# A folded matrix stored by partition, a single row's products moved back, and two order edges in the opening

## The chip, the cores and the metric

The kernel runs on one core of one Trainium2 chip. The metric is device microseconds of one execution, from the median of several runs. The engines are called as in the profile: PE (TensorE, matmuls), ACT (ScalarE), DVE (VectorE), POOL (GpSimd) and SP (SyncE, which issues nearly all DMAs).

## The reference

One step of a two-layer backbone on 256 context tokens and 1024 latent tokens (10 tiles of 128) of width 1024. Each layer normalises its input, modulates it by shift and scale from the condition, mixes, gates and adds:

```
h = modulate(rms_norm(x, g), shift, scale)      # shift, scale, gate = silu(c) @ W_ada + b
even layer: p = h @ W_in; mixer A global GQA, mixer B windowed GQA with a sink,
            x = x + gate * ([silu(gA)*A, silu(gB)*B] @ W_out)
odd layer:  u = h @ W_u; Y = Re(FFT2(u over positions and each group's 256 channels))
            x = x + gate * ((silu(g) * Y) @ W_out)
```

Layer 0 is even, layer 1 odd; a last RMS norm gives the outputs, beside the new keys and values. All is float32.

## The kernel before, in words

All matrix products are made of a high and a low half of each operand, rounded so that PE takes them in its faster float32 form: three matmuls per product (hi·hi, hi·lo, lo·hi; `mm3`, L262 to L271). A raw float32 tile is cast to its high half on ACT or DVE (L290, L292) and the low half is a subtraction on DVE or POOL (L296); the helper is `split`.

The Fourier layer's transform over channels is folded into the weight ahead of time: W_u times the Fourier matrix of a group (tiles `wa`, L575). That product is written in the opening to a DRAM tensor `wd` and read back late, in the u stage. `wd` is laid out as [2, 1024, 2, 256]: half, row of the matrix, group, column. `fold_put` (L563 to L565) writes four 128-row blocks at a time; each partition gets pieces of 1 KB, which lie 2 KB apart from one partition to the next.

**The opening** (0 to about 70 us). Four `warm` matmuls on zeros (L233) come first. Then PE folds `wa`, computes the chunks `ada0` to `ada3` of the condition's linear map (L488), transposes normalised x tiles (`xt`, L445) and begins the first projections (`kv..s`, L544, and `q`, L271). The order in which the program issues these steps is a list of codes written by hand, `PH0` and `S1`; a scheduler sorts each engine's instructions from there by their waits. The steps that matter here:

- `N1` (`norm_rows`, L433 to L439): for each x tile of the second token group, ACT squares it and sums the squares (L433), DVE and POOL make the reciprocal root for two tiles at a time (`n11rx`, L248, `n11ry`, L250), and DVE scales the rows (L439).
- `A1` (`ada_chunk`, L488 to L529): 32 matmuls of a chunk, then ACT copies the resulting row from PSUM (L529). `M1` (`ada_fin`) has PE transpose that row (`modt`, L534) and DVE add and multiply it into `modb` and `moda` (L500, L505, L506).
- `Y2` (`mod_chunk`, L452 to L460): a transposed chunk of x becomes a modulated high and low half: ACT writes the high one (L458), DVE the full value (L459) and the difference (L460).
- `s1`: the splits of the weight `w1` (`w_in`), whose raws are `h` tiles: casts at L292, differences at L296.

SP's DMAs use eight semaphores in turn, and an issue waits until the DMA eight before it has landed.

**The u stage** (about 970 to 1000 us). For each of the two halves of `wd`, `u_load` reads four raw tiles per half and column part (L1565, two DMAs each of 128x2x129 or 128x2x128), splits them, and PE computes blocks `u00` to `u04`, then `u10` to `u14`, of 24 matmuls of 128x258 each (L271). One token position stands alone (the Nyquist row); its products with the same raw tiles are `xr`, 16 matmuls per half in four groups of four (L1578). A raw tile's buffer is free once its high half, low half and `xr` group have read it.

Of the kernel before, what the change touches and what calls it, by code (L numbers as in the profile page):

```python
# [9 lines left out]
F32 = mybir.dt.float32  # L10
# [3 lines left out]
AF = mybir.ActivationFunctionType  # L14
ALU = mybir.AluOpType
AX = mybir.AxisListType

P = 128
D = 1024
# [32 lines left out]
USES = ((0,), (1,), (2, 3), (2, 3), (4, 7), (6, 7), (4, 6), (5,), (8,), (9,))  # L52
BETWEEN = {(8, 1): [("E", k) for k in range(3)], (9, 0): [("E", k) for k in range(3, 8)], (9, 1): [("O", k) for k in range(2)]}
OPRE = 2
WARM = 4
BEHIND = {7: 5}
ROWS_BEHIND = (9,)
PW1 = "11111"
# [84 lines left out]
def hybrid_step(ctx: ExitStack, tc: tile.TileContext, I, O):  # L143
    nc = tc.nc
    pe, act, dve, pool, sp = nc.tensor, nc.scalar, nc.vector, nc.gpsimd, nc.sync
# [44 lines left out]
    vd = dr.tile([2, NT, P, P], F32, name="vd")  # L190
    od = dr.tile([NT, P, 8, P], F32, name="od")
    gd = dr.tile([NT, P, 8, P], F32, name="gd")
    wd = dr.tile([2, D, 2, 256], F32, name="wd")
    x1d = dr.tile([NT * P, D], F32, name="x1d")
    g1d = dr.tile([8, P, NT * P], F32, name="g1d")
    scd = dr.tile([NT, 2, 8, P], F32, name="scd")
# [67 lines left out]
    def mm3(out, terms, lo=0, hi=None):  # L264
        n = 3 * len(terms)
        hi = n if hi is None else hi
        i = 0
        for lh, ll, rh, rl in terms:
            for a, b in ((lh, rh), (lh, rl), (ll, rh)):
                if lo <= i < hi:  # L270
                    pe.matmul(out, a, b, start=i == 0, stop=i == n - 1)  # L271
                i += 1

    turn = {}
    lows = {}
# [11 lines left out]
    def copy(key, cycle, out, in_):  # L287
        e = pick(key, cycle)
        if e is act:
            return act.activation(out, in_, AF.Copy)  # L290
        else:
            e.tensor_copy(out, in_)  # L292

    def split(dst_h, dst_l, src, hc="a", lc="p"):
        copy("hi" + hc, hc, dst_h, src)
        return pick("lo" + lc, lc).tensor_sub(dst_l, src, dst_h)  # L296


# [38 lines left out]
    def wk(w, k, c0, n):  # L337
        h, l = w[k // 4]
        return h[:, k % 4, c0 : c0 + n], l[:, k % 4, c0 : c0 + n]
# [111 lines left out]
    def mod_chunk(gi, k, src, full, hh, hl, lc):  # L451
        v = GROUPS[gi][2]  # L452
        sc, sh = moda[:, 0, k, v : v + 1], modb[:, 0, k, v : v + 1]
        if pick("mf", E_MF) is act:
            act.activation(full, src, AF.Identity, bias=sh, scale=sc)
            pick("mh", E_MH).tensor_copy(hh, full)
        else:
            act.activation(hh, src, AF.Identity, bias=sh, scale=sc)  # L458
            dve.tensor_scalar(full, src, sc, sh, op0=ALU.mult, op1=ALU.add)  # L459
        pick("ml" + lc, lc).tensor_sub(hl, full, hh)  # L460

    def h_alloc(gi):
# [57 lines left out]
    def ada_chunk(kk, raws):  # L520
        ps = bank("g", f"ada{kk}")
        for b in range(8):
            for j in range(4):
                part, i = divmod(j, 2)
                raw = raws[b // 4 * 2 + part]
                ada_mm(ps, j, b, raw[:, b % 4, i * P : i * P + P], b == 0, b == 7)
        drop(*raws)
        rows[kk] = take("e", (P, P))
        act.activation(rows[kk].a, ps[:, 0:P], AF.Copy)  # L529

    def ada_fin(kk):
        row = rows.pop(kk)
# [29 lines left out]

    def fold_put(g, r0, src):  # L563
        n = src.shape[1]
        sp.dma_start(wd[g // 2, r0 : r0 + n * P, g % 2, :].rearrange("(k p) f -> p k f", p=P), src)  # L565

    early = {}

# [64 lines left out]
    def first_step(op):  # L633
        nm, i = op[0], int(op[1:])
        if nm == "L":
            ada[i] = ada_load(i, ADA_Z[i])
        elif nm == "S":
            small_loads(i)
        elif nm == "x":
            load_x(i, XZ[i])  # L640
        elif nm == "N":
            norm_rows(i)
        elif nm == "w":
            W[i] = load_w(w0cols((C_KA, C_QA)[i]), lc=LC0, later=w_fin.setdefault(i, []))
        elif nm == "s":
            for fin in w_fin[i]:
                fin()
        elif nm == "f":
            wu0[i] = fold_load(i)
        elif nm == "F":  # L650
            fold_piece(i // 10, i % 10, wu0[i // 10], True)
        elif nm == "G":
            e = early.pop((i // 10, i % 10))
            fold_put(i // 10, i % 10 * 512, e.a)
            drop(e)
        elif nm == "A":
            ada_chunk(i, ada.pop(i))
        elif nm == "M":
            ada_fin(i)
        elif nm == "T":  # L660
            XT[0, i] = x_T(0, i)
        elif nm in "XYZ":
            g = "XYZ".index(nm)
            mod_T(g, i, E_ML[g])
        elif nm in "KR":
            t = 4 * "KR".index(nm)
            gemm_chunk(acc0[t], t, W[0], i)
            gemm_chunk(acc0[t + 2], t + 2, W[0], i)
        else:
            return False  # L670
        return True
# [651 lines left out]
    def eo_cols(key, k, c0, n):  # L1323
        kper = 4 if key == "C" else 2
        hh, hl = EH[key][k // kper]
        return hh[:, k % kper, c0 : c0 + n], hl[:, k % kper, c0 : c0 + n]
# [232 lines left out]

    def u_gap(c, hf):  # L1560
        def fn(raw, r0):
            v = raw.a.rearrange("p j (g f) -> p j g f", g=2)
            cols = slice(0, 129) if c == 0 else slice(128, 256)
            for g in range(2):
                sp.dma_start(v[:, :, g, :], wd[hf, r0 : r0 + 2 * P, g, cols].rearrange("(j p) f -> p j f", p=P))  # L1565
            if c == 1:
                pool.memset(v[:, :, :, 0:1], 0.0)
        return fn

    def u_load(n):  # L1570
        c, hf = divmod(n, 2)
        ps = t_bank(f"xr{hf}") if c == 0 else None

        def row(raw, k0):
            for kk in range(2):
                for h in range(2):
                    j = 2 * kk + h
                    pe.matmul(  # L1578
                        ps[32 * j : 32 * j + 32, 0:130], xo[:, k0 + kk, :], raw[:, kk, 128 * h : 128 * h + 130],
                        start=k0 == 6, stop=k0 == 4,  # L1580
                    )
            if k0 == 4:
                act.activation(xsum[hf].a, ps[:, 0:130], AF.Copy)

        if c == 0:
            return load_w(None, width=258, tags=("u", "w", "p"), gap=u_gap(c, hf), each=row)
        return load_w(None, tags=BIG, gap=u_gap(c, hf))
# [105 lines left out]
    for n in range(4):  # L1693
# [60 lines left out]
        for i in (0, 1, 2, 3, 4):  # L1754
            if i < 4:
                key, c0 = "EO"[c], i * P
            else:
                key, c0 = "C", c * P
            ps = next_bank(f"u{n}{i}")[:, 0:width]
            mm3(ps, [(*eo_cols(key, k, c0, P), *wk(w, k, 0, width)) for k in range(8)])  # L1760
            pv = ps.rearrange("p (g f) -> p g f", g=2)
            for gg in range(2):
                hi, lo = y_at(c, i, 2 * hf + gg)
                act.activation(hi, pv[:, gg, 0:P], AF.Copy)
                dve.tensor_sub(lo, pv[:, gg, 0:P], hi)
            if c == 0:
                dve.tensor_copy(nyr[:, i, 2 * hf : 2 * hf + 2].unsqueeze(2), pv[:, :, P : P + 1])
            if n == 3 and i in AT_F:
                fine_part(AT_F.index(i))
# [242 lines left out]
```

## Time and profile before

| | us |
|---|---|
| median of 3 runs | 1184.28 (1183.18 to 1186.94) |
| profiled execution, its own time | 1181.38 |
| its span, first to last instruction | 1179.6 |
| PE busy | 1152.3 |
| DVE busy | 834.6 |
| ACT busy | 570.6 |
| POOL busy | 327.9 |

The profile is of one execution. Busy time counts an engine's own instructions; PE's is the sum that the end of the kernel follows most closely, so the reading below goes by the places at which PE waits. In a timeline row the first number is the start in us from the span's beginning, the second the duration; then engine, line of the source, operation, what it writes and reads, the count of instructions merged in the row, and in brackets the idle time before it with the instruction that ended it.

### The profile page before, as it was taken

How to read it: one execution, taken by the hardware profiler on the slowest of the kernel's cores; microseconds unless marked ns; L12 is line 12 of the kernel's file. 1: busy time of each engine (PE TensorE's matmuls, PEld its weight loads, DVE VectorE, ACT ScalarE, POOL GpSimd, SP SyncE). 2: the span in 40 equal slices, each digit the busy share in tenths (PEclk: the TensorE clock that was granted, in tenths of full speed). 3: DMA queues.
4: the chain of work that ended last, by engine and by line, in shares of the span. 5: the costliest groups of instructions: out<-in, count | busy, mean ns of one | idle time of the engine just before them, and what ended most of it. 6: DMA issues, size and time to landing. Idle time of an engine off the chain costs nothing.

```text
span 1179.6 us, 22036 instructions
## 1 busy us (share of the span) xinstructions
PE 1152.3 (98%) x8111; PEld 1033.8 (88%) x8111; DVE 834.6 (71%) x1995; ACT 570.6 (48%) x1149; POOL 327.9 (28%) x293
## 2 busy tenths in 40 slices
PE   9999999999999999999999989999999999999997
PEld 7787999999999998899988888888777889998886
DVE  3479787877677776668888968886765963468543
ACT  4343465566556555556776665532363234342211
POOL 2345644511322221010110035366221236100001
PEclk9999999999999999999999999999999999999999
DMA  9968412223523232255253487784214426264321
GB/s 367 370 240 270 153 54 76 88 83 99 162 68 102 77 96 76 79 126 134 71 155 89 133 230 222 234 253 161 90 45 145 150 98 195 85 218 141 125 108 54
DMA packets 112848, 168.81 MB, mean 143 GB/s; under 512 B 26202, under 2 KB 63830, under 8 KB 112740
## 3 DMA queue, kind: packets, MB, share of 16 engines
q1 hardware_dynamic: 110228, 158.74, 42.9%
q0 software_dynamic: 2368, 8.39, 2.3%
q8 instruction: 64, 1.05, 0.4%
q14 instruction: 44, 0.36, 0.1%
q10 hardware_dynamic: 144, 0.26, 0.1%
HBM read 123.19 MB, written 44.16 MB: 142 GB/s over the span
## 4 chain that ended last, share of the span: by engine, by line
PE 73%; DMA 11%; DVE 7%; issue 3%; ACT 2%; POOL 2%; SPq 1%; POOLq 0%; DVEq 0%; ACTq 0%
PE of L271 9%; PE av L1071 9%; PE pt L1065 8%; PE q L271 8%; PE ga L271 8%; PE sL L946 5%; PE u L271 4%; PE g1O L271 4%; PE oz L271 3%; PE g1E L271 3%; PE sC L946 3%; PE kv L271 2%; PE g1c L271 2%; DMA u<-i_x 2%; DMA wd<-u 2%
## 5 line engine op out<-in xcount | busy, mean ns | idle before, releaser
L1068 DVE TENSOR_TENSOR pt<-pt,pt 128x512 fp32r<-128x512 f32 (+1 forms) x264 | 171.2, 658 | 41.5 <-ACT pt L290 40.5
L290 ACT ACTIVATE pt<-pt 128x512 fp32r<-128x512 f32 (+1 forms) x265 | 147.2, 576 | 101.1 <-PE pt L1065 55.6
L1071 PE MATMUL av<-pt,u 128*128 128x256 f32 x1008 | 167.1, 288 | 0.7 <-ACT pt L290 0.6
L1065 PE MATMUL pt<-identr,p 128*128 128x128 f32 x1008 | 155.2, 272 | 0.6 <-ACT p L987 0.3
L271 PE MATMUL q<-w,u 128*128 128x256 f32 x960 | 143.2, 287 | 0.0
L1071 PEld LDWEIGHTS av<-pt,u 128*128 128x128 f32 x1008 | 138.7, 189 | 4.9 <-ACT pt L290 0.8
L271 PEld LDWEIGHTS q<-w,u 128*128 128x128 f32 x960 | 126.8, 189 | 5.2 <-issue 0.6
L987 ACT ACTIVATE p<-p,nm 128x1280 f32<-128x1280 f32 (+1 forms) x80 | 95.5, 1194 | 63.0 <-DVE p L980 62.4
L1065 PEld LDWEIGHTS pt<-identr,p 128*128 128x128 f32 x1008 | 119.1, 140 | 7.1 <-PE sB L1018 0.6
L271 PE MATMUL ga<-u,w 128*128 128x512 f32 (+1 forms) x576 | 124.5, 361 | 0.8 <-DVE byp L1042 0.5
L271 PEld LDWEIGHTS ga<-u,w 128*128 128x128 f32 x576 | 93.8, 188 | 15.1 <-ACT pt L290 1.2
L296 POOL TENSOR_TENSOR w<-h,w 128x512 fp32r<-128x512 f32 x38 | 50.7, 1351 | 130.4 <-DVE w L292 101.0
L946 PE MATMUL sL<-u,q 128*128 128x512 f32 x256 | 82.5, 409 | 0.0
L987 ACT ACTIVATE p<-p,NM 128x640 f32<-128x640 f32 (+2 forms) x80 | 59.2, 740 | 33.4 <-DVE p L980 33.2
L946 PE MATMUL sC<-u,q 128*128 128x256 f32 x320 | 62.8, 295 | 1.2 <-DMA q<-qd 0.6
L980 DVE TENSOR_SCALAR_CACHE_REDUCE p<-sL 128x512 f32<-128x512 f32 x64 | 43.8, 685 | 24.6 <-PE sL L946 15.1
L721 POOL TENSOR_TENSOR h<-h,rope 128x512 f32<-128x512 f32 (+1 forms) x18 | 21.8, 1212 | 125.8 <-ACT h L804 77.2
L271 PE MATMUL oz<-u,w 128*128 128x512 f32 x192 | 55.9, 396 | 0.3 <-DVE w L296 0.3
L980 DVE TENSOR_SCALAR_CACHE_REDUCE p<-sL,nm 128x512 f32<-128x512 f32 x64 | 47.7, 745 | 10.3 <-PE sL L946 9.5
L946 PEld LDWEIGHTS sC<-u,q 128*128 128x128 f32 x320 | 48.5, 189 | 4.7 <-DVE e L1082 1.0
L296 POOL TENSOR_TENSOR u<-h,u 128x512 fp32r<-128x512 f32 x16 | 21.0, 1323 | 110.1 <-ACT u L290 83.4
L271 PE MATMUL of<-u,u 128*128 128x512 f32 x150 | 48.2, 393 | 0.0
(730 smaller groups left out, 2598.5 us busy)
## 6 DMA issues: line engine op xcount, KB each, us to landing
q<-qd SPq DMA_DIRECT2D x80, 256.0 KB
h<-i_w_in SPq DMA_DIRECT2D x40, 256.0 KB
h<-i_w_out SPq DMA_DIRECT2D x32, 256.0 KB
p<-i_ada_s SPq DMA_DIRECT2D x11, 512.0 KB
qd<-pt SPq DMA_DIRECT2D x20, 256.0 KB
qd<-q SPq DMA_DIRECT2D x18, 256.0 KB
w<-i_wuT SPq DMA_DIRECT2D x8, 512.0 KB
u<-i_x SPq DMA_DIRECT2D x8, 512.0 KB
```

Of the source, the lines that this page charges most:

```text
L271: pe.matmul(out, a, b, start=i == 0, stop=i == n - 1)
L290: return act.activation(out, in_, AF.Copy)
L296: return pick("lo" + lc, lc).tensor_sub(dst_l, src, dst_h)
L721: pick("rope", XE["rope"]).tensor_mul(t1.rearrange("p t h (b c) -> p t (h b) c", b=2), y.rearrange("p t h (b c) -> p t (h b) c", b=2), cb)
L946: pe.matmul(ps, q_at(q, s, hc), keys, start=s == 0, stop=s == 1)
L980: dve.tensor_scalar(p[i][:, end[i] : end[i] + n], ps, sign, last[i], op0=ALU.mult, op1=ALU.min, accum_out=c)
L987: act.activation(p[i][:, 0 : end[i]], p[i][:, 0 : end[i]], AF.Exp, bias=last[i], scale=-1.0, accum_out=SU[:, t, hd + i, 0:1],)
L1065: pe.transpose(tp[:, jj * 256 + i * P : jj * 256 + i * P + P], p[i][:, off : off + P], ident)
L1068: dve.tensor_sub(pt[:, 1, 0:n], tp[:, 0:n], pt[:, 0, 0:n])
L1071: pe.matmul(acc, vv, pt[:, s, jj * 256 : jj * 256 + 256], start=c + jj + s == 0, stop=c + jj == nt - 1 and s == 1,)
```

## The change

Five edits, made together.

1. `WARM` goes from 4 to 6: two more matmuls on zeros at the start.
2. `wd` is laid out as [2, 128, 8, 2, 256]: half, partition, row block, group, column. The writes hold the same bytes and pieces; a partition's share of a half is now one stretch of 16 KB. `u_gap` loads a raw tile by one DMA of 128x4x129 (or 128) instead of two of 128x2x129: 16 loads instead of 32, with the same pieces of about 512 bytes.
3. The single row's products stand on PE behind the last matmul of block `u03` (first half) and `u11` (second half). `queue_behind` sets the order on an engine without adding a semaphore.
4. In the opening, ACT's copy of chunk 1's row stands behind the square of x tile (1,1).
5. In the opening, DVE's full value of the modulated chunk (1,2) stands behind the last cast of `w1`.

The helpers `mm3`, `copy`, `split` and `mod_chunk` return or remember the instructions that the order is hung on.

```diff
-WARM = 4
+XROW_BEHIND = ((0, 3), (1, 1))
+WARM = 6
...
-    wd = dr.tile([2, D, 2, 256], F32, name="wd")
+    wd = dr.tile([2, P, 8, 2, 256], F32, name="wd")
...
     def split(dst_h, dst_l, src, hc="a", lc="p"):
-        copy("hi" + hc, hc, dst_h, src)
+        lows["hi"] = copy("hi" + hc, hc, dst_h, src)
...
-            dve.tensor_scalar(full, src, sc, sh, op0=ALU.mult, op1=ALU.add)
+            lows["mc", gi, k] = dve.tensor_scalar(full, src, sc, sh, op0=ALU.mult, op1=ALU.add)
...
-        act.activation(rows[kk].a, ps[:, 0:P], AF.Copy)
+        cp_ = act.activation(rows[kk].a, ps[:, 0:P], AF.Copy)
+        if kk == 1:
+            queue_behind(cp_, lows["sq", 1, 1])
...
-        sp.dma_start(wd[g // 2, r0 : r0 + n * P, g % 2, :].rearrange("(k p) f -> p k f", p=P), src)
+        sp.dma_start(wd[g // 2, :, r0 // P : r0 // P + n, g % 2, :], src)
...
         elif nm == "s":
             for fin in w_fin[i]:
                 fin()
+                if i == 1:
+                    queue_behind(lows["mc", 1, 2], lows["hi"])
...
-            v = raw.a.rearrange("p j (g f) -> p j g f", g=2)
             cols = slice(0, 129) if c == 0 else slice(128, 256)
-            for g in range(2):
-                sp.dma_start(v[:, :, g, :], wd[hf, r0 : r0 + 2 * P, g, cols].rearrange("(j p) f -> p j f", p=P))
+            rows = wd[hf, :, r0 // P : r0 // P + 2, :, cols].rearrange("p j g f -> p (j g) f")
+            sp.dma_start(raw.a.rearrange("p j (g f) -> p (j g) f", g=2), rows)
...
-                    pe.matmul(
-                        ps[32 * j : 32 * j + 32, 0:130], xo[:, k0 + kk, :], raw[:, kk, 128 * h : 128 * h + 130],
-                        start=k0 == 6, stop=k0 == 4,
+                    xrow_mm[hf].append(
+                        pe.matmul(
+                            ps[32 * j : 32 * j + 32, 0:130], xo[:, k0 + kk, :], raw[:, kk, 128 * h : 128 * h + 130],
+                            start=k0 == 6, stop=k0 == 4,
+                        )
                     )
...
-            mm3(ps, [(*eo_cols(key, k, c0, P), *wk(w, k, 0, width)) for k in range(8)])
+            last = mm3(ps, [(*eo_cols(key, k, c0, P), *wk(w, k, 0, width)) for k in range(8)])
+            if (n, i) in XROW_BEHIND:
+                for mm in xrow_mm[n]:
+                    queue_behind(mm, last)
```

The order of instructions on an engine shows what moved. First ACT in the opening, before: `e_471<-ada_438` is the copy of chunk 1's row, the lines L433 are the squares of the second group's x tiles (u_299 to u_302).

```order
22 L455 ACTIVATE h_371<-xt_360,modb,moda 128x512
23 L433 ACTIVATE h_389,n10q<-u_299 128x1024
24 L529 ACTIVATE e_471<-ada_438 128x128
25 L433 ACTIVATE h_391,n10q<-u_300 128x1024
26 L433 ACTIVATE h_402,n12q<-u_301 128x1024
27 L433 ACTIVATE h_404,n12q<-u_302 128x1024
```

And now, with line numbers two higher and buffer numbers two higher:

```order
22 L457 ACTIVATE h_373<-xt_362,modb,moda 128x512
23 L435 ACTIVATE h_391,n10q<-u_301 128x1024
24 L435 ACTIVATE h_393,n10q<-u_302 128x1024
25 L531 ACTIVATE e_473<-ada_440 128x128
26 L435 ACTIVATE h_404,n12q<-u_303 128x1024
27 L435 ACTIVATE h_406,n12q<-u_304 128x1024
```

The copy stands one square later. On DVE the first addition of `modt` (modb) follows it: before it stood ahead of the two row scalings at L439, now behind them.

Second, DVE at `w1`, before: `h_650` is the full value of chunk (1,2), `u_644` its low half, and the casts L292 of h_571 to h_579 are the high halves of `w1`.

```order
46 L460 TENSOR_TENSOR u_526<-h_532,u_525 128x512
47 L459 TENSOR_SCALAR h_650<-xt_645,moda,modb 128x512
48 L292 CAST w_569<-h_571 128x512
49 L292 CAST w_569<-h_573 128x512
50 L460 TENSOR_TENSOR u_644<-h_650,u_643 128x512
51 L292 CAST w_575<-h_577 128x512
52 L296 TENSOR_TENSOR w_570<-h_573,w_569 128x512
53 L292 CAST w_575<-h_579 128x512
54 L500 TENSOR_TENSOR modb<-modt_659,bT 128x4
```

And now:

```order
46 L462 TENSOR_TENSOR u_528<-h_534,u_527 128x512
47 L294 CAST w_571<-h_573 128x512
48 L294 CAST w_571<-h_575 128x512
49 L298 TENSOR_TENSOR w_572<-h_575,w_571 128x512
50 L294 CAST w_577<-h_579 128x512
51 L294 CAST w_577<-h_581 128x512
52 L461 TENSOR_SCALAR h_652<-xt_647,moda,modb 128x512
53 L462 TENSOR_TENSOR u_646<-h_652,u_645 128x512
54 L502 TENSOR_TENSOR modb<-modt_661,bT 128x4
```

All four casts stand ahead of the chunk's two instructions.

Third, PE in the u stage, before: `xr_12106` is the first half's single row; u_12190, u_12222, u_12252 and u_12282 are the blocks u00 to u03, u_12119 and u_12120 the high and low halves of the raws w_12121 and w_12126.

```order
4961 L271 MATMUL u_12282<-u_12120,u_10896 128x258
4962 L271 MATMUL u_12282<-u_12119,u_10897 128x258
4963 L1578 MATMUL xr_12106<-w_12126,e_12088 32x130 x4
4964 L1578 MATMUL xr_12106<-pt_12109,e_12088 32x130 x4
4965 L1578 MATMUL xr_12106<-q_12114,e_12088 32x130 x4
4966 L1578 MATMUL xr_12106<-w_12121,e_12088 32x130 x4
4967 L271 MATMUL u_12190<-u_12119,u_10920 128x258
4968 L271 MATMUL u_12222<-u_12119,u_10920 128x258
4969 L271 MATMUL u_12252<-w_12107,w_10817 128x258
```

And now, where u_12276 is block u03 and u_12306 block u04:

```order
5005 L272 MATMUL u_12276<-u_12120,u_10922 128x258
5006 L272 MATMUL u_12276<-u_12119,pt_10923 128x258
5007 L1586 MATMUL xr_12108<-w_12125,e_12090 32x130 x4
5008 L1586 MATMUL xr_12108<-pt_12111,e_12090 32x130 x4
5009 L1586 MATMUL xr_12108<-q_12115,e_12090 32x130 x4
5010 L1586 MATMUL xr_12108<-w_12121,e_12090 32x130 x4
5011 L272 MATMUL u_12306<-w_12109,u_11078 128x258
5012 L272 MATMUL u_12306<-u_12110,u_11078 128x258
```

The row's products stand behind the end of blocks u00 to u03 instead of in their midst. On POOL the two low halves of the tile pair u_12338 (2.53 us in the trace of before under the name u<-h x2) now stand ahead of the low half u_12120 of w_12121, and on SP the loads of the second half's raws pt, q and w wait for the row's products to have read the old tiles.

More of the change, by code (lines that the diff above doesn't have):

```diff
@@ L270, in mm3 @@
                 if lo <= i < hi:
-                    pe.matmul(out, a, b, start=i == 0, stop=i == n - 1)
+                    last = pe.matmul(out, a, b, start=i == 0, stop=i == n - 1)
                 i += 1
+        return last
     turn = {}
@@ L291, in copy @@
         else:
-            e.tensor_copy(out, in_)
+            return e.tensor_copy(out, in_)
     def split(dst_h, dst_l, src, hc="a", lc="p"):
-        copy("hi" + hc, hc, dst_h, src)
+        lows["hi"] = copy("hi" + hc, hc, dst_h, src)
         return pick("lo" + lc, lc).tensor_sub(dst_l, src, dst_h)
@@ L1561, in fn @@
         def fn(raw, r0):
-            v = raw.a.rearrange("p j (g f) -> p j g f", g=2)
             cols = slice(0, 129) if c == 0 else slice(128, 256)
-            for g in range(2):
-                sp.dma_start(v[:, :, g, :], wd[hf, r0 : r0 + 2 * P, g, cols].rearrange("(j p) f -> p j f", p=P))
+            rows = wd[hf, :, r0 // P : r0 // P + 2, :, cols].rearrange("p j g f -> p (j g) f")
+            sp.dma_start(raw.a.rearrange("p j (g f) -> p (j g) f", g=2), rows)
             if c == 1:
-                pool.memset(v[:, :, :, 0:1], 0.0)
+                pool.memset(raw.a.rearrange("p j (g f) -> p j g f", g=2)[:, :, :, 0:1], 0.0)
         return fn
+    xrow_mm = ([], [])
     def u_load(n):
```

## The prediction

> **What bounds the kernel now.** I read the page's busy shares first, then the table of windows, then the timeline of the engine that is busiest, and only then the other engines at the places where that one stands still. The first line gives busy time, share of the span and instructions.
>
> ```profile
> PE 1152.3 (98%) x8111; PEld 1033.8 (88%) x8111; DVE 834.6 (71%) x1995; ACT 570.6 (48%) x1149; POOL 327.9 (28%) x293
> ```
>
> Of a span of 1179.6 us PE stands still for 27.3, so an edit that leaves PE's arithmetic alone can win only where those 27 us lie, or where PE runs below its clock. The windows show where (each row: window, its length, busy us of PE, PEld, DVE, ACT and POOL with counts, granted clock, DMA share, GB/s).
>
> ```profile
> 30.00:50.00 20.00, 18.08 (x263) 14.93 (x252) 9.07 (x23) 9.35 (x17) 6.40 (x5) 1.00 1.04 406
> 50.00:60.00 10.00, 9.73 (x120) 7.98 (x118) 6.38 (x10) 1.33 (x3) 3.75 (x3) 1.00 0.82 290
> 60.00:70.00 10.00, 8.37 (x68) 8.00 (x69) 6.64 (x12) 5.85 (x9) 5.41 (x5) 1.00 0.97 377
> 70.00:100.00 30.00, 30.00 (x373) 27.40 (x376) 26.28 (x73) 14.12 (x29) 13.15 (x16) 1.00 0.62 207
> 100.00:130.00 30.00, 26.91 (x362) 23.36 (x353) 25.87 (x61) 7.02 (x16) 19.82 (x18) 1.00 0.74 241
> ```
>
> PE loses 1.9, 0.3 and 1.6 us in the windows from 30 to 70, nothing from 70 to 100, 3.1 after 100. DMA is full from 30 to 50 us (1.04), so no load there can come sooner. PE's timeline names the stops of the opening (start, duration, work, then in brackets the idle time and who ended it).
>
> ```profile
> 1.26 3.78 PE L233 MATMUL warm<-e 128*128 128x256 f32 x8 [1.26 <-DVE ones L209]
> 5.57 6.73 PE L575 MATMUL wa<-h,w 128*128 128x256 f32 x19 [0.53 <-DMA w<-i_wuT]
> ...
> 40.95 0.41 PE L445 MATMUL xt<-identr,u 128*128 128x128 f32 x2 [1.75 <-DVE moda L505]
> ...
> 56.80 0.73 PE L544 MATMUL kv4s<-w,u 128*128 128x256 f32 x4 [0.24 <-DVE u L460]
> ...
> 61.40 0.66 PE L445 MATMUL xt<-identr,u 128*128 128x128 f32 x4 [1.44 <-ACT h L455]
> ```
>
> Their sum is 3.96 us, and each has one part of the change aimed at it. The other place is the u stage, where the single row's products stop PE twice, both times for a load of the folded matrix.
>
> ```profile
> 984.52 0.43 PE L1578 MATMUL xr<-w,e 128*32 128x130 f32 x8 [0.76 <-DMA w<-wd]
> ...
> 992.27 0.43 PE L1578 MATMUL xr<-w,e 128*32 128x130 f32 x8 [0.59 <-DMA w<-wd]
> ```
>
> That is 1.35 us more. The whole prize is about 5.3 us of idle time, plus what an earlier full clock at the start is worth.
>
> **The change part by part.** *Two more warm matmuls.* The folded matrix's first pieces go to ACT at these times.
>
> ```profile
> 9.36 0.60 ACT L290 ACTIVATE u<-wa 128x512 f32<-128x512 f32 x1 [7.02 <-PE wa L575]
> 11.69 0.60 ACT L290 ACTIVATE u<-wa 128x512 f32<-128x512 f32 x1 [1.74 <-PE wa L575]
> 13.42 0.60 ACT L290 ACTIVATE u<-wa 128x512 f32<-128x512 f32 x1 [1.13 <-PE wa L575]
> ```
>
> A piece takes 1.73 us once PE is fast (11.69 to 13.42); the one before took 2.33, so part of it ran slow. The granted clock reads 1.00 in the windows, but the pieces say otherwise: if slow means half speed, the 2.33 us piece was slow for its first 2 x (2.33 - 1.73) = 1.20 us. That ends at 9.36 + 1.20 = 10.56, less ACT's lag behind PE, for which I put 0.14, an estimate: PE became fast at 10.42. That is 4.85 us after 5.57, where the unbroken run of work begins; the warm run ahead of it had been cut by the 0.53 us gap. Four warm matmuls take 3.78 us, so six reach from 1.26 to 6.93 at half speed, past the landing at 5.57, and there is no gap. By the same 4.85 us PE is fast from 6.11, the last 0.82 us of warm work shrink to 0.41, and wa starts at 6.52. Before, 4.85 us at half speed were 2.42 us of full-speed work, done at 10.42; now they are done at 6.52 + 2.42 = 8.94. Gain 1.5 us. If full speed comes no sooner, the two matmuls cost half of 3.78 less the gap's 0.53: 1.4 us lost. If PE were fast from 5.04, where the old warm run ended, wa would start at 5.99 and the gain be 2.0. I take 1.5, by the only row there is, and keep -1.4 and 2.0 as ends. The Trainium skill, "TensorE: Matmul & The Clock Gate", section "Part 1: The HAM clock gate", says that the gate goes from half to full rate after one busy window of 3.4 us, that the windows run freely, and that the point moves from run to run. By that rule windows would have ended here at 7.0 and 10.4, the gap spoilt the first, and the gain would be about 1.0; the rows agree with a step near 10.4, and the phase in other executions no run here shows.
>
> *Edge A, ACT's copy of chunk 1's row behind the square of x tile (1,1).* The chain ahead of the 1.75 us stop runs through ACT and then DVE.
>
> ```profile
> 33.98 1.05 ACT L433 ACTIVATE h<-u 128x1024 bf16<-128x1024 f32 x1
> ...
> 36.17 0.28 ACT L529 ACTIVATE e<-ada 128x128 f32<-128x128 f32 x1 [1.05 <-PE ada L488]
> 36.34 1.05 ACT L433 ACTIVATE h<-u 128x1024 bf16<-128x1024 f32 x1
> ```
>
> ```profile
> 37.52 0.17 DVE L248 TENSOR_SCALAR n11rx<-n10q 128x2 f32<-128x2 f32 x1 [2.32 <-ACT h L433]
> 39.24 0.16 DVE L500 TENSOR_TENSOR modb<-modt,bT 128x4 f32<-128x4 f32 x1 [1.55 <-PE modt L534]
> 39.32 1.42 DVE L439 TENSOR_SCALAR u<-u,n11ry 128x1024 f32<-128x1024 f32 x2
> ```
>
> The copy waits 1.05 us for PE while the second square stands behind it; then modb waits 1.55 us on DVE for modt while the two row scalings, which PE needs, stand behind that. With the edge the second square runs right after the first, at about 35.0 instead of 36.34, and in the new order modb comes behind the scalings: they can start about 1.3 us sooner and no longer wait for PE at all. Scalings at about 38.0 to 39.4 give PE its tiles by 39.5, against 40.95, so I take 1.4 of the 1.75. What is next: the copy itself, delayed by at most one square's 1.05 us, which is less than what it waited. Bounds: 0 if the x tile lands no sooner than its square ran, 1.75 if all goes.
>
> *Edge B, the modulation of (1,2) behind the casts of w1.* DVE stands 6.11 us for ACT's evicted chunk and then has everything at once.
>
> ```profile
> 53.59 0.81 DVE L459 TENSOR_SCALAR h<-xt,moda,modb 128x512 f32<-128x512 f32 x1 [6.11 <-ACT u L458]
> 54.31 0.75 DVE L292 CAST w<-h 128x512 fp32r<-128x512 f32 x2
> 54.98 1.77 DVE L460 TENSOR_TENSOR u<-h,u 128x512 fp32r<-128x512 f32 x1
> ...
> 59.04 0.15 DVE L500 TENSOR_TENSOR modb<-modt,bT 128x4 f32<-128x4 f32 x1
> 59.29 1.19 DVE L506 TENSOR_TENSOR moda<-moda,gT 128x4 f32<-128x4 f32 x1
> ```
>
> The casts now run in the idle 6.11 us, if w1's raws have landed: they are issued ahead of the wd writes and of x's last tiles, inside the full stream up to 50 us. The modb and moda, at 59.0 to 60.5, no longer stand behind them, and PE's 1.44 and 0.24 us waits for them go. I take 1.7, with 0 to 1.7 as ends. The wait that the edge adds: the modulation stands behind the last raw's cast, so a late raw would hold the u halves that kv4s and kv6s read; the raw would have to land after 53.5 to do so.
>
> *What is late next.* Everything after now runs 4.6 us sooner (1.5, 1.4 and 1.7), but the loads don't. The first of the last x tiles is issued here, has landed by the eighth issue after it (SP's issues wait for that), and is squared on ACT here:
>
> ```profile
> 47.57 0.33 SPq L424 DMA_DIRECT2D pt<-i_x  x1
> ...
> 58.99 1.41 SPq L871 DMA_DIRECT2D q<-i_ada_s  x1
> ```
>
> ```profile
> 62.78 1.04 ACT L433 ACTIVATE h<-pt 128x1024 bf16<-128x1024 f32 x1
> ```
>
> The square moves from 62.78 to about 58, when the tile may not have landed, and ACT would stand there half a microsecond with PE's evictions behind it; I put 0.5 for this and 0.3 for chunk 2's raws, estimates, and 0 to 2 as ends. From 70 to 100 us PE is full (30.00 of 30.00), so the shift carries; DVE with 26.28 of 30 has 3.7 us to spare there.
>
> *Folded matrix by partition, sixteen fewer loads, the row's products later.* PE's arithmetic is the same. The two stops of 0.76 and 0.59 us were at the row's products; those now stand behind u03 and u11, past the loads. What takes their place: ACT's hi and POOL's lo of the same raws.
>
> ```profile
> 980.66 1.11 SPq L1565 DMA_DIRECT2D w<-wd  x2
> 987.21 0.93 SPq L1565 DMA_DIRECT2D pt<-wd  x2
> ```
>
> ```profile
> 990.07 0.64 ACT L290 ACTIVATE u<-pt 128x516 fp32r<-128x516 f32 x1 [3.22 <-DMA pt<-wd]
> ```
>
> ```profile
> 980.18 1.29 POOL L296 TENSOR_TENSOR u<-w,u 128x516 fp32r<-128x516 f32 x1 [3.75 <-DMA h<-wd]
> 981.47 2.53 POOL L296 TENSOR_TENSOR u<-h,u 128x512 fp32r<-128x512 f32 x2
> ```
>
> A pair of issues costs SP 1.1 us at 980.66, so one DMA instead of two lets the raw land about half a microsecond to a microsecond sooner. But POOL now does the pair of 2.53 us ahead of the 1.29 us one; the lo half of the raw w comes at about 984, and PE, which by then has done the blocks' first halves, stands about 0.65 us for it. So of 1.35 I keep 0.7, with 1.35 and -2 as ends. Behind the row's products (0.43 us rows, about 0.9 us in all) nothing on PE waits for them; but the next raws can be loaded only when they have read the old ones, about 990.4 instead of the 987.21 at which pt was issued. From there 990.07 - 987.21 = 2.9 us to ACT's hi: at 993.3, and block u04 and the halves of u1x that need only the earlier raw cover PE until about 994.8. Slack 1.5 us.
>
> The sum: 1.5 + 1.4 + 1.7 - 0.8 + 0.7 = 4.5 us. The profiled execution took 1181.38 us (the span and 1.8 around it) and would take 1176.9; it lies 2.9 under the median of the runs, 1184.28, to which the forecast is put: 1179.8.
>
> **The rivals.** *The opening is given back (no difference that can be measured).* Against the saturated DMA (1.04 from 30 to 50 us) each stop that goes uncovers the next landing, and after 100 us PE waits 3.1 us in 30 with DVE at 25.87: DVE or a load may set the pace there whatever came before. For it: that DMA share. Against: PE's unbroken 70 to 100. If half of the opening's 3.8 us is lost so, the gain is 2.6: 1181.7. With the clock no sooner as well (2.9 worse) it is gone: 1184.6.
>
> *Everything goes (faster still).* Full clock at 5.04 gives 2.0, both edges take their whole idle time, no new wait: 2.0 + 1.75 + 1.7 + 1.35 = 6.8, 1177.5. The chance is small, since five things must hold.
>
> *Slower: rows of the folded matrix 16 KB apart.* One partition's block of wd is now 16 KB from the next instead of 2 KB, for writes and loads, with the same pieces of 1 KB and 512 bytes. The writes stand in SP's queue here.
>
> ```profile
> 48.81 7.54 SPq L565 DMA_DIRECT2D wd<-u  x4
> ```
>
> In 50 to 60 us, where they run, the stream falls from 406 to 290 GB/s, so such pieces are the slow ones already. If the new pitch doubled these 7.5 us, the adaLN weights queued behind them (p, pt and q from i_ada_s) come 7.5 us later, and the PE stops after 100 us grow by that: -4.5 + 7.5 = 3.0 slower, 1187.3. It decides from writes 60% longer (4.5 of 7.54). For it only the fall in that window; against it, bytes and pieces are the same, so I hold it unlikely. The Trainium skill, "DMA: Bandwidth & Descriptors", section "Latency and other measured facts", reports lost rate for row pitches that are large powers of two, measured from 512 KB up; 16 KB lies far below, and no run here shows it.
>
> A second way to lose is the u stage: raws more than 1.5 us later than in my walk make PE wait, and each microsecond over costs one; it would need over 6 to make the kernel slower.
>
> **How the numbers follow.** My forecast, 3 to 6 us gained, gets 0.57; the opening given back in part or in whole 0.28; everything goes 0.05; slower, by the pitch or the u stage, 0.10. About 0.3% (3.55 us) is what a measurement of this kernel can tell from no change, so faster means under 1180.7 and slower over 1187.8. Nine tenths of the forecast and all of "everything goes" are faster (0.56); of the slower case, whose price starts near 3 us and has no upper end, most is over the bound (0.08); the rest, 0.36, is no difference. For the range I go down to the case in which everything goes and 1 us under it, since the runs themselves lie up to 3.8 us apart: 1176.5; and up to 1185.0, which holds the opening given back. The slower case and a little at the lower end stay out.
>
> **What would show it.** Right: ACT's first evictions of wa all 1.73 us apart from the second on, and the first near 8.3 instead of 9.36; no stop of over 0.5 us at the xt transposes near 38 and 57; casts of w1 on DVE before 53; the first wait at 70 us reached about 4 us sooner; the row's products without a wait, and a short stop for POOL's lo before them. Wrong: a first eviction after 9.4 (no earlier clock); stops at the xt transposes as long as before; PE waits from 100 to 130 us that grow by as much as the opening won; hi casts of the u stage's second raws after 995; or wd writes that hold SP for over 10 us.

## The result, and the profile after

The changed kernel took 1179.85 us in the median of 21 runs (1176.32 to 1183.57), the kernel before 1182.26 (1178.36 to 1189.56) in as many on the same chip: a ratio of 0.9972, 95% interval 0.996 to 0.9984, or 1.9 to 4.7 us. The forecast was 1179.8 from a median of 1184.28. So total and sign came out; several of the steps behind them did not.

The profiled execution has a span of 1177.2 us against 1179.6. These are PE's rows in its timeline that answer to the stops of before; the columns are start, duration, work, and idle time ahead with its releaser.

```profile
1.26 5.49 PE L234 MATMUL warm<-e 128*128 128x256 f32 x12 [1.26 <-DVE ones L210]
...
30.76 0.66 PE L447 MATMUL xt<-identr,u 128*128 128x128 f32 x4
...
39.08 0.41 PE L447 MATMUL xt<-identr,u 128*128 128x128 f32 x2 [0.42 <-DVE moda L507]
...
54.56 1.69 PE L272 MATMUL q<-w,u 128*128 128x256 f32 x12 [0.47 <-ACT e L531]
...
64.03 0.33 PE L538 MATMUL modt<-identr,e 128*128 128x128 f32 x1 [0.22 <-ACT h L457]
...
100.05 0.70 PE L272 MATMUL kv<-w,u 128*128 128x256 f32 x3 [0.70 <-DVE u L462]
...
126.57 0.64 PE L490 MATMUL ad<-q,e 128*32 128x128 f32 x16 [2.06 <-DMA q<-i_ada_s]
...
980.04 0.62 PE L272 MATMUL u<-u,u 128*128 128x258 f32 x3 [0.99 <-ACT u L292]
...
987.94 0.43 PE L1586 MATMUL xr<-w,e 128*32 128x130 f32 x8
```

Before, the same rows began at 31.26, 40.95, 67.79 (the modt), 103.81 (the kv) and 128.72 us (the ad). So the lead is 0.5 us at the first x transposes, 1.9 behind the old 1.75 us stop, 3.8 at 64 us and still 3.8 at 100 us; then one wait of 2.06 us for an adaLN weight, which before did not exist, brings it down to 2.1. It is about 2.0 at 960 us and 2.4 at the end. The stops of 1.75, 0.24 and 1.44 us have become 0.42 and 0.47, and the row's products wait for nothing; in their place the blocks wait 0.99 us for ACT.

### The profile page after: what moved, and what is told of

It is laid out like the page before. It is cut to its first block, busy times and chain, and to the rows that moved or that the text cites. A ratio compares the mean times of both kernels' runs of the same rounds, so it can differ in the third digit from the quotient of the medians.

```text
span 1177.2 us, 22017 instructions
## 1 busy us (share of the span) xinstructions
PE 1151.5 (98%) x8115; PEld 1033.7 (88%) x8115; DVE 833.5 (71%) x1995; ACT 570.2 (48%) x1149; POOL 328.2 (28%) x293
## 3 DMA queue, kind: packets, MB, share of 16 engines
q8 instruction: 64, 1.05, 0.4%
## 4 chain that ended last, share of the span: by engine, by line
PE 71%; DMA 12%; DVE 8%; issue 3%; ACT 2%; POOL 2%; SPq 0%; POOLq 0%; DVEq 0%; ACTq 0%
PE of L272 9%; PE av L1077 9%; PE ga L272 9%; PE pt L1071 8%; PE q L272 8%; PE sL L952 5%; PE u L272 5%; PE g1O L272 3%; PE sC L952 3%; PE g1E L272 2%; PE kv L272 2%; DMA u<-i_x 2%; PE g1c L272 1%; DMA q<-i_ada_s 1%; DMA od<-e 1%
## 5 line engine op out<-in xcount | busy, mean ns | idle before, releaser
L292 ACT ACTIVATE pt<-pt 128x512 fp32r<-128x512 f32 (+1 forms) x265 | 147.2, 576 | 99.9 <-PE pt L1071 55.8
```

## The experiments

Twelve kernels, each with one or some of the five edits or with one exchange of its own, timed in turn with the kernel before. The table has what their profiles say of the opening: how many warm matmuls; the start of ACT's first eviction of `wa`; the start of PE's first x transposes; the stop of PE ahead of the second group's first transposes; the granted clock from 40 to 42 us; the start of the last of the opening's `modt`; and the ratio of times to the kernel before (95% interval). Times in us.

| kernel | warm | eviction | xt | stop | clock | modt | ratio |
|---|---|---|---|---|---|---|---|
| before | 4 | 9.36 | 31.26 | 1.75 | 1.00 | 67.79 | 1 |
| changed | 6 | 8.60 | 30.76 | 0.42 | 1.00 | 64.03 | 0.9972 (0.996-0.9984) |
| e1 warm only | 6 | 8.18 | 30.41 | 0.41 | 1.00 | 65.59 | 0.9990 (0.9974-1.0007) |
| e2 both edges only | 4 | 7.07 | 28.37 | 1.75 | 0.50 | 64.53 | 0.9991 (0.9973-1.0010) |
| e3 opening only | 6 | 8.74 | 30.90 | 0.41 | 1.00 | 64.16 | 0.9971 (0.9957-0.9986) |
| e4 u stage only | 4 | 6.79 | 28.40 | 1.75 | 0.50 | 66.19 | 0.9982 (0.9964-1.0000) |
| e5 changed, four warm | 4 | 6.91 | 29.19 | 1.75 | 1.00 | 63.83 | 0.9979 (0.9959-0.9999) |
| e6 edge A only | 4 | 7.30 | 28.80 | 1.75 | 0.50 | 66.78 | 0.9998 (0.9980-1.0015) |
| e7 edge B only | 4 | 6.93 | 28.23 | 1.75 | 0.55 | 64.06 | 0.9987 (0.9968-1.0006) |
| e8 other adaLN buffers | 6 | 8.55 | 30.71 | 0.42 | 1.00 | 63.96 | 0.9996 (0.9979-1.0013) |
| e9 exchange only | 4 | 7.34 | 28.89 | 2.04 | 0.50 | 67.13 | 0.9986 (0.9968-1.0004) |
| e10 four warm, exchange | 4 | 7.11 | 28.42 | 0.88 | 1.00 | 62.19 | 0.9971 (0.9950-0.9991) |
| e11 row's products only | 4 | 6.96 | 29.27 | 1.75 | 1.00 | 65.81 | 1.0006 (0.9986-1.0025) |
| e12 layout only | 4 | 6.93 | 28.23 | 1.95 | 0.50 | 66.36 | 1.0001 (0.9981-1.0021) |

The intervals are about as wide as the effects, so the ratios tell only the ends of the list apart; the rest is read from the profiles, one execution each. Every lead below is counted against the one profile of before, and that one began late: the nine other kernels with four warm matmuls stand 2.0 to 3.0 us ahead of it at the first x transposes. A lead in a profile is therefore not a share of the measured time.

**e1, six warm matmuls alone.**

```diff
-WARM = 4
+WARM = 6
```

> The kernel before with six warm matmuls instead of four and nothing else. Theory (the opening's gains carry, less what interleaving and landings take back): PE's full clock comes near 6.6 us instead of 10.4, the first eviction of wa near 8.6 instead of 9.36, the shift is about 1.4 us at 12 us and some 0.5 left when the first x transposes start near 31 us; time 0.3 to 0.8 us under before. Rival (the opening is covered by landings, so only the u stage counts): the same early shift, nothing left of it at 100 us, time equal to before. Second rival (the warm matmuls are the whole gain): 2 us or more under before.

The lead at the first transposes was 0.85 us, and behind the old stop it was 2.2, since the stop had shrunk to 0.41 without any edge; the ratio, 0.9990, is not clear of 1. Two warm matmuls also exchange instructions of other engines: the rows of DVE and ACT here stand as in the changed kernel, ACT's copy behind the second square and modb behind the row scalings. What the prediction credits to edge A is already there. DVE's rows in e1, where the scalings (L439) run ahead of modb (L500) and moda (L505), the two additions that read modt:

```profile
36.38 1.42 DVE L439 TENSOR_SCALAR u<-u,n11ry 128x1024 f32<-128x1024 f32 x2 [0.88 <-POOL n11ry L250]
38.36 0.16 DVE L500 TENSOR_TENSOR modb<-modt,bT 128x4 f32<-128x4 f32 x1 [0.56 <-PE modt L534]
38.44 0.15 DVE L505 TENSOR_TENSOR moda<-modt,bT 128x4 f32<-128x4 f32 x1
```

**e2, both edges alone.**

```diff
+            queue_behind(cp_, lows["sq", 1, 1])
...
+                    queue_behind(lows["mc", 1, 2], lows["hi"])
```

> The kernel before with the two order edges in the opening and nothing else (four warm matmuls, old layout, old loads, row's products where they were). Theory: PE's waits of 1.75, 0.24 and 1.44 us go down to about 0.9 in all, the shift is about 2.7 to 3.2 us from 62 to 115 us, up to 1.6 of it may be lost at one adaLN load near 125 us; time 1.2 to 3 us under before. Rival (the opening is covered by landings): the waits go but the shift is below 0.5 us after 130 us; time within 0.5 of before.

The stop stayed at 1.75 us, against the expectation, and more was lost behind it than the stop explains. Of the lead of 2.9 us at 31 and at 38 us, nothing should go until edge B adds to it, yet the modt leads only by 3.3. The windows of the granted clock show it; here of e4, which has the same stop (each row: window, length, busy us of PE, PEld, DVE, ACT, POOL, granted clock, DMA share, GB/s).

```profile
36.00:40.00 4.00, 2.18 (x13) 1.44 (x13) 2.96 (x10) 2.60 (x4) 0.70 (x1) 0.83 1.03 404
40.00:42.00 2.00, 2.00 (x20) 1.64 (x22) 2.00 (x4) 0.00 (x0) 0.46 (x1) 0.50 1.04 418
42.00:44.00 2.00, 2.00 (x35) 1.44 (x28) 0.06 (x1) 0.71 (x2) 1.19 (x1) 0.99 1.04 424
```

And of the changed kernel, without the stop:

```profile
36.00:40.00 4.00, 3.42 (x29) 2.78 (x27) 2.05 (x9) 2.85 (x6) 1.33 (x2) 1.00 0.98 390
40.00:42.00 2.00, 2.00 (x30) 1.70 (x34) 2.00 (x3) 0.62 (x1) 0.06 (x1) 1.00 1.04 420
42.00:44.00 2.00, 2.00 (x31) 1.44 (x22) 1.18 (x4) 0.94 (x2) 1.47 (x1) 1.00 1.01 413
```

A PE that looks full (2.00 of 2.00) did 20 matmuls at clock 0.50 where the other did 30 at 1.00. The same six transposes took 1.48 us in e4 and 0.87 in the changed kernel:

```profile
40.03 1.48 PE L447 MATMUL xt<-identr,u 128*128 128x128 f32 x6
```

```profile
40.67 0.87 PE L447 MATMUL xt<-identr,u 128*128 128x128 f32 x6
```

Of the nine kernels with a stop of 1.75 us or more, six have such a dip behind it (e2, e4, e6, e7, e9, e12) and three do not (before, e5, e11); of the five with 0.88 or less, none. The cost is the time from the stop's end to the last modt: without edge B 26.84 us in before, 26.86 in e1 and e11, but 28.10 to 28.30 in e4, e6, e9 and e12; with edge B 24.94 to 24.95 in five kernels, but 26.47 and 26.15 in e2 and e7. A dip costs 1.2 to 1.5 us on top of the stop.

The traces also hold the times at which the granted clock changed. In all six the fall comes 34.13 us after the clock was first granted in full, which is ten times 3.413 us, and it lasts 3.413 us. Counted in stretches of that length, PE had worked 0.2 to 1.2 us between the start of the stretch and the stop in the six with a dip, and 1.4 to 1.5 us in the three without. That may be what decides; nine profiles only suggest it, and no run set it apart.

**e3, the opening's three edits; e4, the u stage's two.** Both are the changed kernel with the other half as before.

```diff
-WARM = 4
+WARM = 6
...
+            queue_behind(cp_, lows["sq", 1, 1])
...
+                    queue_behind(lows["mc", 1, 2], lows["hi"])
```

> Six warm matmuls and both edges, old layout of the folded matrix, old loads, row's products where they were. Theory: the shift is about 3.8 us from 62 to 115 us as in the changed kernel, and the time is 2 to 3 us under before. If the new layout slowed the opening's writes, this kernel is faster in the opening than the changed one and waits less for the adaLN load near 125 us. Rival (only the u stage counts): within 0.5 us of before.

> The new layout, half the loads and the row's products moved back, with the opening as before (four warm matmuls, no edges). Theory: no shift up to 970 us; in the u stage the waits of 0.76 and 0.59 us at the row's products go and about 1 us for POOL's or ACT's halves comes; time 0.3 to 0.7 us under before. Rival (the u stage is the whole gain): 2 to 3 us under before. Rival (the layout costs in the opening what the stage wins): a shift to later of over 0.5 us already at 130 us.

e3 has the whole gain within its interval (0.9971), and its lead at 64 us, 3.6, is the changed kernel's. e4's ratio, 0.9982, has an interval that reaches 1.0000, so it shows no gain of the stage. In e4's profile a lead of 2.9 us is there at the first transposes, with an opening like before's: PE became fast early in this execution, as in all with four warm matmuls but before's. Across the u stage, from 960 to 1020 us, its lead went from 1.5 to 1.35.

**e5, the changed kernel with four warm matmuls; e6 and e7, one edge each.**

```diff
-WARM = 6
+WARM = 4
```

> The changed kernel with four warm matmuls instead of six. First four profiles with four warm matmuls or six gave the clock's step at very different times (four: 10.6, 5.6, 5.3 us; six: 7.1, 6.3, 7.5), so theory: the step comes at a point that differs from execution to execution, four warm matmuls can be lucky (first x transposes near 28.4 us) or unlucky (near 31.3), six lie between (30.4 to 30.9); averaged over executions the two extra matmuls are worth little, time within 1 us of the changed kernel. Rival (six are worth what the first pair of profiles showed): 0.5 to 1.5 us slower than the changed kernel, and a step near 10.5 us again.

> The kernel before with ACT's copy of chunk 1's row behind the square of x tile (1,1), nothing else. Theory (x tiles' landing near 33 to 36 us sets that stop, not the copy's place, when PE comes early): with an early clock step the stop stays near 1.8 us and the edge is worth 0 to 0.3; with a late step it falls to about 0.4 and the edge is worth 1.3. Time 0 to 1 us under before. Rival (my prediction's step): the stop falls by 1.3 us in any case, time 1.4 under before.

> The kernel before with the modulation of (1,2) behind w1's casts, nothing else. Theory: the 1.44 us stop for ACT at the xt transposes and the 0.24 us stop go, a new wait of about 0.5 us for ACT's copy of chunk 2's row may come; the shift between 50 and 65 us grows by 1.2 to 1.7 us; time 0.8 to 1.7 under before. Rival (edge B's gain is taken by the landing of the next x tiles): a shift of under 0.5 us between 45 and 70 us.

e5's ratio, 0.9979, cannot be told from the changed kernel's, 0.9972; but neither can e2's, 0.9991, from e3's, 0.9971, and these two differ by the same two matmuls and lie 2.4 us apart. What the two are worth in time is not settled. e6: edge A alone moves the copy on ACT, and the stop stays at 1.75; what holds it is DVE's order, as the rows below show, and not the landing of the x tiles alone, as I had expected. e7: edge B takes away the stops of 0.24 and 1.44 us, adds 0.47 for ACT's copy of chunk 2's row, and from the stop's end to the modt 26.85 us become 24.95 where no dip disturbs: 1.9 us won, 0.7 more than the stops' difference. DVE's rows show the casts in its idle time, waiting only for the raws:

```profile
47.48 0.43 DVE L294 CAST w<-h 128x512 fp32r<-128x512 f32 x1 [1.85 <-DMA h<-i_w_in]
48.14 1.48 DVE L294 CAST w<-h 128x512 fp32r<-128x512 f32 x1 [0.23 <-DMA h<-i_w_in]
...
51.74 0.81 DVE L461 TENSOR_SCALAR h<-xt,moda,modb 128x512 f32<-128x512 f32 x1 [0.73 <-ACT u L460]
...
56.43 0.16 DVE L502 TENSOR_TENSOR modb<-modt,bT 128x4 f32<-128x4 f32 x1 [2.49 <-PE modt L536]
```

**e9, one exchange on DVE; e10, the changed kernel with four warm matmuls and this exchange.**

```diff
-        mod_shift(0, 2 * kk, 2, tv[:, 0:2])
+        sh_ = mod_shift(0, 2 * kk, 2, tv[:, 0:2])
+        if kk == 1:
+            queue_behind(sh_, lows["sc", 1, 1])
```

Here `lows["sc", 1, 1]` is the second row scaling.

> The kernel before with one pair of DVE instructions exchanged and nothing else: the addition of chunk 1's modt to modb stands behind the two row scalings, as in all kernels with six warm matmuls and in none with four. Theory (this order is what removes the 1.75 us stop, not edge A and not the clock's step at the start): the stop falls to 0.9 us or less, since ACT's copy still stands ahead of the second square, and the granted clock stays at 1.00 from 36 to 48 us, where four of six kernels with the stop fell to 0.5; time 0.8 to 2.3 us under before. Rival (x tiles land too late, so the stop is theirs): the stop stays near 1.75 with another name.

> The changed kernel with four warm matmuls and the same exchange on DVE by a third edge. Theory: with the usual early step (near 5.5 us) the first x transposes come near 28.5 us, the stop is at most 0.5 us, the clock stays up, and the shift at 60 to 100 us is 5 to 6 us against 3.8 in the changed kernel; adaLN loads near 125 us may take 1 to 2 of it; time 0.5 to 2 us under the changed kernel (which took 1179.85 beside 1182.26). Rival (landings of x tiles and weights set the opening whatever PE does): the shift at 100 us is not over 4 us, time as the changed kernel.

With e6 this makes the four cases of two orders. PE's row at the stop in e6 (copy moved), e9 (modb moved) and e10 (both):

```profile
38.48 0.41 PE L447 MATMUL xt<-identr,u 128*128 128x128 f32 x2 [1.75 <-DVE moda L507]
```

```profile
38.87 0.41 PE L445 MATMUL xt<-identr,u 128*128 128x128 f32 x2 [2.04 <-DVE moda L505]
```

```profile
37.24 0.41 PE L447 MATMUL xt<-identr,u 128*128 128x128 f32 x2 [0.88 <-DVE moda L507]
```

The stop ends in every kernel with DVE's moda, which reads modt, and not with the scaled tiles. In e6 modb waits for modt, and the two scalings come between it and moda:

```profile
36.77 0.16 DVE L502 TENSOR_TENSOR modb<-modt,bT 128x4 f32<-128x4 f32 x1 [1.86 <-PE modt L538]
36.85 1.42 DVE L441 TENSOR_SCALAR u<-u,n11ry 128x1024 f32<-128x1024 f32 x2
38.18 0.15 DVE L507 TENSOR_TENSOR moda<-modt,bT 128x4 f32<-128x4 f32 x1
```

This order gives 1.75 in seven kernels and 1.95 in the eighth, e12. With the scalings first, as in e1, the stop is 0.41 or 0.42 in the four with six warm matmuls. e10 differs from e5 by this exchange alone and has 0.88 instead of 1.75, without a dip.

e9 has the exchange and still 2.04 us. At first sight ACT's copy, ahead of the second square there, holds the scalings. ACT's rows say otherwise; e9, then e10:

```profile
33.66 1.06 ACT L433 ACTIVATE h<-u 128x1024 bf16<-128x1024 f32 x1 [1.85 <-DMA u<-i_x]
34.72 0.26 ACT L529 ACTIVATE e<-ada 128x128 f32<-128x128 f32 x1
34.94 1.06 ACT L433 ACTIVATE h<-u 128x1024 bf16<-128x1024 f32 x1
```

```profile
32.03 1.06 ACT L435 ACTIVATE h<-u 128x1024 bf16<-128x1024 f32 x1 [0.79 <-DMA u<-i_x]
33.31 1.06 ACT L435 ACTIVATE h<-u 128x1024 bf16<-128x1024 f32 x1
```

The second square follows the first by 1.28 us with the copy between them and without it, and the stop ends 5.21 us after the first square in both. So the copy cost nothing in e9; its x tile was in use 1.63 us later, and my rival, the late landing, is what happened. The copy itself waits only in before (1.05 us) and e11 (0.45).

e10 had the expected lead of 5.6 us at 64 us and 100 us, and ended with 2.2. The adaLN loads took 0.8 of it; in this execution there was also a stop of 2.80 us at 690 us with a dip of the clock to 0.50 behind it. Its ratio, 0.9971, is the changed kernel's: no better version is shown.

**e8, other buffers for the late adaLN loads.**

```diff
-        raw = take(AT_Z, (P, 2, 512))
+        raw = take(AT_Z if (l, part, h) != (1, 1, 1) or s == 0 else ("p", "pt"), (P, 2, 512))
```

> The changed kernel with the last three adaLN weight tiles of the attention layer's list put in p and pt buffers only, so that none waits for a query tile's store before its load is issued. Theory (the opening's gain is given back near 125 us because that load is issued 6.7 us before PE wants it, behind a store): the wait of 2.06 us goes, the shift stays near 3.7 us beyond 130 us, time 0.5 to 1.6 us under the changed kernel. Rival (the stream of weights as a whole is late, whichever buffer): a wait of 1 to 2 us at one of the three tiles stays, time as the changed kernel. Third possibility: the query tiles' reloads come later for it and the next stage waits instead.

The wait did not go but moved to the other two tiles, with a dip behind the second:

```profile
123.27 0.64 PE L490 MATMUL ad<-p,e 128*32 128x128 f32 x16 [1.84 <-DMA p<-i_ada_s]
127.29 0.65 PE L490 MATMUL ad<-pt,e 128*32 128x128 f32 x16 [1.11 <-DMA pt<-i_ada_s]
```

```profile
130.00:132.00 2.00, 2.00 (x8) 1.61 (x8) 1.26 (x4) 0.00 (x0) 0.00 (x0) 0.50 0.03 12
```

The lead of 3.8 us became a lag of about 2 us (2.2 at 500 us), and the gain was lost (0.9996). PE also uses these tiles sooner here, so this does not settle whether the stream or the buffer is late; that stays open.

**e11 and e12, the u stage's edits one by one.** e11 has `XROW_BEHIND` with the old `wd` and two loads per tile, e12 the new layout and one load.

```diff
-    wd = dr.tile([2, D, 2, 256], F32, name="wd")
+    wd = dr.tile([2, P, 8, 2, 256], F32, name="wd")
```

> The kernel before with the single row's products behind blocks u03 and u11, with the old layout and two loads per tile. Theory (the u stage waits for the same load wherever its first reader stands): the stops of 0.76 and 0.59 us at the row's products go, a stop of 0.7 to 1.4 us for ACT's or POOL's half of the same tile comes a few us earlier; the shift across 970 to 1010 us is within 0.5 us of nothing. Rival (my prediction's step, 0.7 us won): the shift grows by 0.5 to 1 us there.

> The kernel before with the folded matrix by partition and one load per tile, the row's products where they were. Theory: the tile's issue comes about 1 us sooner, but it lands at nearly the same time, since one load of four blocks takes longer than one of two; the row's products still wait, 0.5 to 1 us; shift across 970 to 1010 us within 0.5 us of nothing; no change in the opening's writes. Rival (half the loads is the gain): the row's stops fall below 0.3 us and the shift grows by 1 us.

The tile w is issued sooner and by one DMA, but in the changed kernel it is in use 4.8 us after its issue and before it was 3.6 (975.85 to 979.47). From the changed kernel's SP and ACT:

```profile
974.51 0.39 SPq L1570 DMA_DIRECT2D w<-wd  x1
```

```profile
979.35 0.63 ACT L292 ACTIVATE u<-w 128x516 fp32r<-128x516 f32 x1 [3.81 <-DMA w<-wd]
```

In e11 the row's stops go and one of 1.45 us for the high half of another raw, q, comes in their place; the lead falls by 1.4 us across the stage.

```profile
986.54 0.63 ACT L292 ACTIVATE u<-q 128x516 fp32r<-128x516 f32 x1 [0.97 <-DMA q<-wd]
```

```profile
987.23 0.39 PE L272 MATMUL u<-u,w 128*128 128x258 f32 x1 [1.45 <-ACT u L292]
```

In e12 the row's products wait for nothing either, against my expectation, and PE stops 1.08 us for ACT's high half of w instead; the lead falls by 0.1.

```profile
980.92 0.63 PE L272 MATMUL u<-u,u 128*128 128x258 f32 x3 [1.08 <-ACT u L292]
```

Across the stage (the lead at 1020 us less that at 960, by PE's rows) the kernels with both edits, the changed one, e4, e5, e8 and e10, came to 0.0 in the mean (from 0.4 won to 0.2 lost); the kernels with the stage as before, e1, e2, e3, e6, e7 and e9, lost 0.4 in the mean with before's own 0 counted in, three of them 0.8 to 0.9. The other four of these lie within 0.13 of nothing, so the means differ by about 0.4 us but the two groups overlap. By e11 the moved products need the single load, and by e12 they add nothing to it that can be seen.

## Why the prediction was right, and which steps were not

*Two more warm matmuls (1.5 us won): wrong as a general gain.* In this pair the step nearly came: the second eviction of `wa` began 1.37 us sooner, at 10.32 instead of 11.69. But the step used one profile, whose first eviction at 9.36 us is the only late one of the ten with four warm matmuls; the other nine have 6.79 to 7.34, and those with six 8.18 to 8.74. By the record of the granted clock that each trace keeps, PE first had full clock at 10.42 us in before, where the prediction had put it, at 4.25 to 5.76 in the other nine with four, and at 5.95 to 7.09 with six. The Trainium skill, "TensorE: Matmul & The Clock Gate", section "Part 1: The HAM clock gate", says that the point varies by about half a microsecond either way, with where the free-running window lies; here it varies, but by about 6 us between profiles with four warm matmuls. Before is also the only one in which PE stood 0.53 us for the first weight behind the warm matmuls (0.22 at most in the others), which fits the gap that the prediction blames; no run set that gap by itself.

First transposes: 28.9 us in the mean of ten with four, 30.7 in the four with six, so the matmuls cost 1.8 us at that place. Part of it is PE's order: with six it takes 20.4 to 20.5 us from the second eviction to the first transposes, with four 19.6 to 19.9 in eight of ten, for the same matmuls without a stop (in the other two PE stands 0.7 us). With six the `ada` matmuls come in four groups among those of `wa`, with four in two; no run changed that order by itself. In the pair the 1.37 us had become 0.5 by then.

*Edge A (1.4 us): the size was right, the cause was not.* The stop fell by 1.34 us. The prediction had PE wait for the scaled tiles; it waited for moda, and the order that frees moda, scalings ahead of modb, comes in the changed kernel from the warm matmuls' effect on the schedule (e1). Edge A with four of them leaves the stop (e5, e6). So the warm matmuls earn there what they lost: behind the stop the kernels with six stand at 39.0 us, and the nine with the stop at 38.7 in the mean. The early start is in part spent on loads: ACT's first square waits 0.49 to 1.92 us for its x tile in nine of the ten with four, and not at all with six. What the six earn beyond is that no dip follows: 1.2 to 1.5 us in six of nine. In the prediction this price of the stop is missing altogether, since before's one profile has the stop without the dip.

*Edge B (1.7 us): right,* 1.9 measured. *What is late next (0.8):* 0.47, at ACT's copy of chunk 2's row, not at the x tiles.

*The u stage (0.7): mis-sized.* It won 0.4 us in this pair and about 0.4 in the mean, which the spread of the profiles does not confirm. The single load was in use no sooner than the two, so a stop of 0.99 us for ACT's half stands where I had 0.65 for POOL's.

*The rivals.* The opening given back holds in part: 1.6 of 3.8 us at one adaLN load in this pair of profiles, and 0.1 to 1.1 in the others (e8 apart). The slower case is out: the four writes of `wd` hold SP 7.10 us against 7.54, and 6.9 to 8.0 over all kernels with no difference by layout.

The sum then reads, as an estimate from these profiles: 0.3 lost at the stop's end, dips saved 0.9 on average (six of nine at 1.35), edge B 1.9, u stage 0.4, less 0.7 at the adaLN loads (the mean of the twelve): 2.2 us, within the measured 1.9 to 4.7. How the measured time divides among the parts is not shown by the ratios. They show that the opening's three edits together have the whole gain within the interval (e3), and that no part alone is clear of no change. The forecast's time was met by luck in part: its 4.5 us were counted from a median of three runs that lay 2.0 above that of 21, a term that holds for one odd profile is in it, and the dips are not.

## What to carry to other kernels

Price a stop of PE by what the granted clock does behind it as well as by its own length, and look at that in several profiles: stops of 1.75 to 2.04 us cost 3 us or more in six of nine profiles. Do not build a term on the start of one execution. And where a scheduler sorts the program, run each edit alone before crediting it, since an edit in one place exchanged the instructions that mattered in another. When an experiment misses, look at which row waited first: in e9 it was a load, not the order that the edit had changed.

## What the runs showed of the hardware that was not expected

The granted clock fell to 0.50 behind stops of only 1.75 to 2.04 us, for 3.41 us each time, in six of nine profiles. In the first 10 us of before the windows read 1.00 although evictions lie 2.33 us apart and then 1.73: the trace has no record of the clock ahead of 10.42 us. One load of 128x4x129 was in use 4.8 us after its issue, where two of 128x2x129 were both in use 3.6 us after the first one's issue; what else stood in the queue was not held the same.
